# A two-layer hybrid decoder trunk on one core: one subtraction in place of two for the weight sums, three more weight units by seven products, and a convolution tap added by DMA

## The chip, the cores and the metric

The kernel runs on one core of a Trainium2 chip. The metric is the device time of one execution in microseconds (us), given as the median of several runs. Lower is better.

The engines' names in the profile are: PE is TensorE's matmuls and PEld its weight loads, DVE is VectorE, ACT is ScalarE, POOL is GpSimd, SP is SyncE. Each engine works through its own list of instructions in order and waits on semaphores of the others. DMAs issued by SP and POOL run on 16 DMA engines.

## The reference

The input is one sequence of 256 tokens with 2048 features, in float32. Layer 0 mixes tokens by causal pooling, layer 1 by an attention that merges three dilated branches. After each mixer come a residual with a layer norm, a gated feed-forward part with a causal convolution of width 3, and again a residual with a layer norm. The change touches the feed-forward part (in both layers) and the weight units that attention's value projection and the down projections share:

```python
def conv_ffn(h, w_up, conv_w, conv_b, w_down):
    S = h.shape[1]
    u = h @ w_up
    up = jnp.pad(u, ((0, 0), (CONV_WIDTH - 1, 0), (0, 0)))
    c = conv_b + up[:, 0:S] * conv_w[0]
    for j in range(1, CONV_WIDTH):
        c = c + up[:, j:j + S] * conv_w[j]
    gate, val = jnp.split(c, 2, axis=-1)
    return (jax.nn.silu(gate) * val) @ w_down
```

The inner width is 5504, that is 43 blocks of 128. All weights together are some 380 MB, and each is read once.

## The kernel before

**Weight units.** All weights go through one list, `units`. A unit is a piece of 512 x 512 of a weight matrix (1 MB; a few have 384 rows or columns). `run_units` works through the list. For unit i, `ahead(i)` first issues the load of a unit further on (SP, three tiles `raw`) and the splitting of unit i + 3, then the matmuls of unit i are issued, then what is due from `later`, then the unit's closing work.

**High and low parts.** Matmuls take their operands in a rounded form of float32. To keep precision, each weight tile is split into a high part `wh` (a cast on ACT) and a low part `wl` (the tile less its high part, a subtraction on DVE), and each product is the sum of three: high by high, high by low and low by high. A plain unit is one cast of 128 x 2048 (L99) and one subtraction (L100). There are four tiles each for `wh` and `wl`, so the splitting of a unit waits until the unit four before it has been used.

**Seven products.** In many units of the down projections and of attention's value projection, `group_tm` computes the unit's product as a 2 x 2 block product with seven block products instead of eight (`mk_seven`). Each of the seven is 2 steps of 3 matmuls of 256 columns: 42 matmuls. A plain unit of these stages is 24 matmuls of 512 columns (`go_t`, L255 to L257). A seven-product unit stands in the list as two entries, "a" (18 matmuls) and "b" (24), and both are made from one loaded tile by `split_sums`:

- "a": a cast of three quarters of the tile (L119); on DVE a difference of weight blocks (L120), the low part (L121), a second difference (L122), and the last one, over half of the tile (L124). The differences overwrite `raw`.
- "b": the overwritten tile is split again, in two halves of 128 x 1024: a cast on ACT (L113) and a subtraction on DVE (L114) for each. The first half needs L120 and L122, the second L124.

There are 72 such units before the change. `sevens` in `ffn` says which blocks q of the down projection are taken so, and for which of the four output blocks c.

**Feed-forward.** The inner blocks are taken four at a time: q = 0 to 10, the last with three. `up(q)` gives four units for the gate half and four for the value half. When the gate's last unit is through, `gate_chain` moves the result to SBUF (`evac`), and `conv` makes the convolution: the last tap with its bias on ACT (L616), then `second` one unit later and `third` two units later, each a tap on ACT (L621) and an addition on DVE (L622). Then the Silu (L644) follows on ACT, one unit after `third`. The value half goes the same way, and `valued` multiplies the two (L702). The tiles `u`, `c`, `a` and `f` share four buffers.

The down projection comes in chunks. Chunks 0 and 1 (three blocks q each) are woven between the units of `up`: in rounds of four plain units and three seven-product units, one round for each output block c. Chunk 2 has two blocks, and its two units for one c stand behind four units of `up`. The last chunk of layer 0 is done in feature order without seven products; that of layer 1 (`down(3, True)`) has blocks 8, 9 and 10.

The results of the seven-product groups are put together by DVE (L845 to L876) and then, in part, added onto the output by two accumulating DMAs of 256 KB each, issued by POOL (L287, `ht<-w`). POOL has few other instructions there. Two other DMAs, L411, accumulate 512 KB each (`h<-cs`).

**Order.** The program is written with `manual_schedule`: the order on each engine is that in which the code issues. `later(n, fn)` holds `fn` back by n entries of the list.

Of the kernel before, what the change touches and what calls it, by code (L numbers as in the profile page):

```python
# [9 lines left out]
F32 = mybir.dt.float32  # L10
# [3 lines left out]
OP = mybir.AluOpType  # L14
# [18 lines left out]
def trunk(ctx: ExitStack, tc: tile.TileContext, x, pool_w_in, pool_w_grp, pool_scale, pool_w_out,  # L33
          attn_w_q, attn_w_o, shared_w_k, shared_w_v, ffn_w_up, ffn_conv_w, ffn_conv_b, ffn_w_down,
          ln1_g, ln1_b, ln2_g, ln2_b, out):
    nc = tc.nc
    V, A, PE = nc.vector, nc.scalar, nc.tensor
# [53 lines left out]
    def do_split(i):  # L91
        if len(units[i]) > 3:
            return split_sums(i, units[i][3])
        r = raw.pop(i)
        shape = [P, r.shape[1], r.shape[2]]
        wh[i] = wp.tile(shape, F32R, name=f"wh{i}", tag="wh")
        wl[i] = wp.tile(shape, F32R, name=f"wl{i}", tag="wl")
        for j, s in enumerate(pieces(i, r.shape[1])):
            A.copy(wh[i][:, s], r[:, s])  # L99
            V.tensor_tensor(wl[i][:, s], r[:, s], wh[i][:, s].bitcast(F32), OP.subtract)  # L100
            if i == 0 and j == 0:
                x_quad(0, (1,))


    B1, B2, N1, N2 = slice(0, 4, 2), slice(1, 4, 2), slice(256, 512), slice(0, 256)

    def split_sums(i, kind):
        h = wh[i] = wp.tile([P, 4, 512], F32R, name=f"wh{i}", tag="wh")
        l = wl[i] = wp.tile([P, 4, 512], F32R, name=f"wl{i}", tag="wl")
        if kind == "b":  # L110
            r = raw.pop(i - 1)
            for n in (N2, N1):
                A.copy(h[:, :, n], r[:, :, n])  # L113
                V.tensor_tensor(l[:, :, n], r[:, :, n], h[:, :, n].bitcast(F32), OP.subtract)  # L114
            return
        r = raw[i]
        r11, r12, r22 = r[:, B1, N1], r[:, B1, N2], r[:, B2, N2]
        hs, ls, rs = (t.rearrange("p (k b) n -> p k (b n)", b=2)[:, :, 256:] for t in (h, l, r))
        A.copy(hs, rs)  # L119
        V.tensor_tensor(r12, r12, r11, OP.subtract)  # L120
        V.tensor_tensor(ls, rs, hs.bitcast(F32), OP.subtract)  # L121
        V.tensor_tensor(r22, r22, r12, OP.subtract)  # L122
        both = r[:, :, N1].rearrange("p (k b) n -> p k b n", b=2)
        V.tensor_tensor(both, both, r22.unsqueeze(2).to_broadcast([P, 2, 2, 256]), OP.subtract)  # L124
# [10 lines left out]
    def later(n, fn):  # L135
        if n == 0:
            fn()
        else:
            pending.append([n, fn])
# [418 lines left out]
    def add_grp(g):  # L558
# [12 lines left out]
             True, 0, 0, after=lambda q: to_tokens(q))  # L571
# [8 lines left out]
    def ffn(lay):  # L580
# [5 lines left out]
        sevens = {q: every for q in range(8)}  # L586
        sets = {0: "C", 1: "A", 2: "B", 3: "C", 4: "A", 5: "B", 6: "A", 7: "CB"[lay], 9: "A"}
        if lay == 1:
            sevens[9] = (0, 2)
        else:  # L590
            sevens[7] = (0, 1)
        free, done = {}, {}

        def pads():
# [4 lines left out]
        def evac(ps, nb, mode):  # L599
            u = pads()  # L600

            if mode == "x":
                norm_evac(ps, nb, lambda m: u[:, m, 2:])
                return u
            for m, n, p in pairs(ps, nb):
                y = u[:, m:m + n, 2:]
                A.copy(y, p[:, :n, T:])  # L607
                V.tensor_tensor(y, y, p[:, :n, :T], OP.add)
            return u

        def conv(u, blk0, nb, then, quick=False):
            cv = cvec[lay]
            c = pools["ffn"].tile([P, 4, T], F32, name="c", tag="t4")
            for m in range(nb):
                j = blk0 + m
                A.activation(c[:, m, :], u[:, m, 2:], AF.Identity, scale=cv[:, 2, j:j + 1], bias=cv[:, 3, j:j + 1])  # L616

            def tap(i, to):
                for m in range(nb):
                    j = blk0 + m  # L620
                    A.activation(to[:, m, :], u[:, m, i:i + T], AF.Copy, scale=cv[:, i, j:j + 1])  # L621
                V.tensor_tensor(c[:, :nb], c[:, :nb], to[:, :nb], OP.add)  # L622

            def second():
                tap(1, pools["ffn"].tile([P, 4, T], F32, name="a", tag="t4"))

            def third():
                tap(0, u[:, :, 0:T])
                then(c)

            for n, fn in ((1, second), (2, third)):
                later(0 if quick else n, fn)

        def gate_post(q, nb, mode):
            def post(ps):
                later(2 if mode == "x" else 0, lambda: gate_chain(q, nb, mode, ps))
            return post

        def gate_chain(q, nb, mode, ps):
                u = evac(ps, nb, mode)  # L640

                def gated(c):
                    def three():
                        A.activation(c[:, :nb], c[:, :nb], AF.Silu)  # L644
                        gates[q] = c

                    later(1, three)

                later(1, lambda: conv(u, 4 * q, nb, gated))

# [44 lines left out]
        def val_chain(q, nb, mode, ps):  # L697
            u = evac(ps, nb, mode)

            def valued(c):  # L700
                s = gates.pop(q)
                V.tensor_tensor(s[:, :nb], s[:, :nb], c[:, :nb], OP.mult)  # L702

                def three():
                    gq[q] = quad_tile("g")
                    split_act(gq[q], s[:, :nb])
                    if q in sevens:
                        left_sums(q, s)

                at(free.get(q, 0), three)  # L710

            after(done.get(q, 0) or state["done"] + (0 if q in (2, 5) or (q == 10 and lay == 0) else 1), lambda: conv(u, NF + 4 * q, nb, valued, q == 10))
# [57 lines left out]
        for n in (0, 1):  # L770
            d = down(n, False)
            q = chunks[n + 1][0]
# [25 lines left out]
    def to_tokens(q):  # L798
        if q == 0:
            ST["hb"] = hp.tile([P, 4, T], F32, name="hb", tag="h")  # L800
        hb = ST["hb"]
        hf = hb.rearrange("p m t -> p (m t)")
        V.transpose(hf.rearrange("p (t m c) -> p m t c", t=2, m=4), H[q].rearrange("p m (t c) -> p m t c", t=2))

        def to():
            HT[q] = hp.tile([P, 4, T], F32, name="ht", tag="h").rearrange("p a t -> p (a t)").rearrange(
                "p (t c) -> p t c", t=2)
            return HT[q].rearrange("p t c -> p (t c)")

        moves(hf, to)  # L810
# [49 lines left out]
    def tm_post(lay, n, c):  # L860
# [92 lines left out]
        return post  # L953

    ffn(0)
    marks.append(len(units))

# [174 lines left out]
    add_last(attn_w_o[0], rows4, [lambda j=j: oq[j] for j in range(4)], True, 1, 0, after=to_tokens)  # L1132
    marks.append(len(units))
    ffn(1)
    marks.append(len(units))

# [34 lines left out]
    with tc.tile_pool(name="pool", bufs=1) as pp:  # L1171
# [5 lines left out]
        for l in range(2):  # L1177
            n = 80 if l == 0 else 64
            r = pp.tile([80, P], F32, name=f"vrow{l}")
# [94 lines left out]
```

## Time and profile before

| | |
|---|---|
| time, median of 3 runs | 2016.33 us (2015.55 to 2018.14) |
| profiled execution, first to last instruction | 2014.9 us |
| PE busy | 2005.8 us |
| DVE busy | 1734.9 us |
| ACT busy | 1269.7 us |
| POOL busy | 93.0 us |
| weight loads of 1 MB from SP, issue to landing | 5.0 to 6.0 us by group (median) |
| accumulating DMAs of 256 KB from POOL (`ht<-w`), 50 | 4.8 us (median) |
| accumulating DMAs of 512 KB from POOL (`h<-cs`), 2 | 11.8 us (median) |
| granted TensorE clock | 1.000 |

The profile has only the span of the execution profiled; the median of the runs is 1.4 us above it. A row of the order of time begins with its start and its length in us, then come the engine, the line, the operation, output and inputs, and in brackets how long the engine had been idle before it and what ended that. A row of the view of groups has count, busy time, mean in ns and idle time ahead. Lines L... are those of the kernel before. The ends of matmuls are modelled, so the time that one takes is read from start to start.

### The profile page before, as it was taken

Reading aid. Unit: us, or ns where it says so; the run is one execution under the profiler, and the core shown is the slowest. Engines: PE = TensorE matmul, PEld = TensorE weight load, DVE = VectorE, ACT = ScalarE, POOL = GpSimd, SP = SyncE. Lnnn points to the kernel's source line nnn. Section 1 sums busy time; section 2 is a strip of 40 time slices with the busy share of each in tenths; the row PEclk is TensorE's granted clock in tenths of the full one; section 3 lists DMA queues with packets and bytes.
Section 4 is the critical chain, followed back from the end, with each engine's and each line's share of the span. In section 5 each row is a group of like instructions: output and inputs, shape, how many; then the busy total and the mean of one; then the engine's idle time right before and its main releaser. Section 6 shows DMA issues by size and latency. Waiting matters only on the chain.

```text
span 2014.9 us, 31474 instructions
## 1 busy us (share of the span) xinstructions
PE 2005.8 (100%) x12760; PEld 1810.2 (90%) x12760; DVE 1734.9 (86%) x1831; ACT 1269.7 (63%) x1551; POOL 93.0 (5%) x153
## 2 busy tenths in 40 slices
PE   9999999999999999999999999999999999999999
PEld 8898988999899988889888988998899989989987
DVE  6868887999899899879896878787899899989899
ACT  6454686767766676657554445487766677667673
POOL 2000000000000000000001021000000000000000
PEclk9999999999999999999999999999999999999999
DMA  8565466666666757885465656557666756666765
GB/s 260 204 208 186 163 212 192 181 221 223 198 198 200 239 179 229 232 230 186 155 220 172 210 172 202 187 188 211 166 224 200 224 186 222 209 211 186 213 208 185
DMA packets 271297, 407.77 MB, mean 202 GB/s; under 512 B 74430, under 2 KB 85588, under 8 KB 270896
## 3 DMA queue, kind: packets, MB, share of 16 engines
q1 hardware_dynamic: 259488, 388.93, 58.8%
q0 software_dynamic: 11232, 16.18, 5.4%
q8 instruction: 100, 1.64, 0.3%
q10 hardware_dynamic: 432, 0.66, 0.1%
q14 instruction: 45, 0.37, 0.1%
HBM read 380.01 MB, written 2.10 MB: 190 GB/s over the span
## 4 chain that ended last, share of the span: by engine, by line
PE 88%; DVE 7%; ACT 2%; DMA 2%; issue 1%; SPq 0%; DVEq 0%; ACTq 0%
PE acc L180 41%; PE acc L181 21%; PE s L244 3%; PE s L246 3%; PE s L245 3%; PE acc L184 2%; PE acc L185 2%; PE acc L183 2%; PE t L246 2%; PE t L244 2%; PE t L245 2%; DVE wl L100 2%; ACT wh L99 1%; DVE wl L114 1%; DVE wl L121 1%
## 5 line engine op out<-in xcount | busy, mean ns | idle before, releaser
L180 PE MATMUL acc<-xc,wh 128*128 128x512 f32 x3264 | 1151.6, 396 | 0.0
L181 PE MATMUL acc<-xc,wl 128*128 128x256 f32 x3264 | 916.2, 281 | 0.8 <-DVE wl L100 0.8
L100 DVE TENSOR_TENSOR wl<-raw,wh 128x2048 fp32r<-128x2048 f32 (+2 forms) x304 | 654.8, 2162 | 171.0 <-ACT wh L99 163.3
L180 PEld LDWEIGHTS acc<-xc,wh 128*128 128x128 f32 x3264 | 616.1, 189 | 142.8 <-issue 0.4
L99 ACT CAST wh<-raw 128x2048 fp32r<-128x2048 f32 (+2 forms) x304 | 546.6, 1805 | 170.8 <-PE acc L180 65.7
L181 PEld LDWEIGHTS acc<-xc,wl 128*128 128x128 f32 x3264 | 615.2, 188 | 1.3 <-DVE wl L100 1.2
L113 ACT CAST wh<-raw 128x1024 fp32r<-128x1024 f32 x144 | 150.7, 1052 | 202.8 <-DVE raw L122 175.5
L114 DVE TENSOR_TENSOR wl<-raw,wh 128x1024 fp32r<-128x1024 f32 x144 | 171.8, 1221 | 11.2 <-ACT wh L113 11.2
L121 DVE TENSOR_TENSOR wl<-raw,wh 128x1536 fp32r<-128x1536 f32 x72 | 126.2, 1753 | 6.3 <-ACT wh L119 5.3
L119 ACT CAST wh<-raw 128x1536 fp32r<-128x1536 f32 x72 | 106.4, 1477 | 36.6 <-PE acc L180 26.5
L287 POOL DMA_DIRECT2D ht<-w x48 | 41.3, 1015 | 1446.4 <-DVE ht L873 720.9
L244 PE MATMUL t<-wh,g 128*128 128x256 f32 x376 | 105.8, 281 | 0.0
L246 PE MATMUL t<-wh,g 128*128 128x256 f32 x376 | 105.7, 281 | 0.0
L245 PE MATMUL t<-wl,g 128*128 128x256 f32 x376 | 105.5, 281 | 0.0
L616 ACT ACTIVATE c<-u,cv 128x256 f32<-128x256 f32 x172 | 89.5, 593 | 23.2 <-DVE f L678 16.5
L246 PE MATMUL s<-wh,xs 128*128 128x256 f32 x344 | 96.1, 279 | 0.0
L244 PE MATMUL s<-wh,xs 128*128 128x256 f32 x344 | 95.9, 279 | 0.0
L245 PE MATMUL s<-wl,xs 128*128 128x256 f32 x344 | 95.9, 279 | 0.0
L124 DVE TENSOR_TENSOR raw<-raw 128x1024 f32<-128x1024 f32 x72 | 88.2, 1225 | 2.4
L621 ACT ACTIVATE a<-u,cv 128x256 f32<-128x256 f32 x172 | 73.5, 500 | 11.9 <-DVE g L688 11.9
L607 ACT COPY u<-acc 128x512 f32<-128x512 f32 x84 | 46.8, 572 | 46.1 <-PE acc L181 45.9
L621 ACT ACTIVATE u<-u,cv 128x256 f32<-128x256 f32 x172 | 73.4, 500 | 0.0
(338 smaller groups left out, 3443.1 us busy)
## 6 DMA issues: line engine op xcount, KB each, us to landing
raw<-in_ffn_w_up_dram SPq DMA_DIRECT2D x160, 1024.0 KB, 5.2
raw<-in_ffn_w_down_dram SPq DMA_DIRECT2D x80, 1024.0 KB, 5.1
raw<-in_pool_w_out_dram SPq DMA_DIRECT2D x16, 1024.0 KB, 5.0
raw<-in_shared_w_k_dram SPq DMA_DIRECT2D x16, 1024.0 KB, 5.2
raw<-in_attn_w_q_dram SPq DMA_DIRECT2D x16, 1024.0 KB, 5.3
raw<-in_shared_w_v_dram SPq DMA_DIRECT2D x16, 1024.0 KB, 5.4
raw<-in_attn_w_o_dram SPq DMA_DIRECT2D x16, 1024.0 KB, 5.2
ht<-w POOLq DMA_DIRECT2D x50, 256.0 KB, 4.8
```

Of the source, the lines that this page charges most:

```text
L99: A.copy(wh[i][:, s], r[:, s])
L100: V.tensor_tensor(wl[i][:, s], r[:, s], wh[i][:, s].bitcast(F32), OP.subtract)
L113: A.copy(h[:, :, n], r[:, :, n])
L114: V.tensor_tensor(l[:, :, n], r[:, :, n], h[:, :, n].bitcast(F32), OP.subtract)
L119: A.copy(hs, rs)
L121: V.tensor_tensor(ls, rs, hs.bitcast(F32), OP.subtract)
L180: PE.matmul(ps[m].ap, h[:, k, c], q[:, k, :, :T], start=st, stop=False)
L181: PE.matmul(ps[m][:, :T], l[:, k, c], q[:, k, 0, :T], start=False, stop=sp)
L244: PE.matmul(to, xh, h[:, k, n], start=opens and kk == 0, stop=False)
L245: PE.matmul(to, xh, l[:, k, n], start=False, stop=False)
L246: PE.matmul(to, xl, h[:, k, n], start=False, stop=ends and kk == 1)
L621: A.activation(to[:, m, :], u[:, m, i:i + T], AF.Copy, scale=cv[:, i, j:j + 1])
```

## The change

Three edits.

1. In `split_sums`, "b" is split by one cast and one subtraction of 128 x 2048 instead of two each of 128 x 1024.
2. In `ffn`, three more units are taken by seven products: block 7 in layer 0 for output blocks 2 and 3, and block 9 in layer 1 for output block 1. There are 75 such units then.
3. In `conv`, for the gate blocks alone, the addition of the third tap (22 in all) is no longer on DVE but an accumulating DMA that POOL issues (512 KB; `u` is read in rows of 1 KB). The Silu is held back by one more unit.

```diff
         if kind == "b":
             r = raw.pop(i - 1)
-            for n in (N2, N1):
-                A.copy(h[:, :, n], r[:, :, n])
-                V.tensor_tensor(l[:, :, n], r[:, :, n], h[:, :, n].bitcast(F32), OP.subtract)
+            A.copy(h, r)
+            V.tensor_tensor(l, r, h.bitcast(F32), OP.subtract)
             return
...
         if lay == 1:
-            sevens[9] = (0, 2)
-        else:
-            sevens[7] = (0, 1)
+            sevens[9] = (0, 1, 2)
...
-        def conv(u, blk0, nb, then, quick=False):
+        def conv(u, blk0, nb, then, quick=False, by_dma=False):
...
-                V.tensor_tensor(c[:, :nb], c[:, :nb], to[:, :nb], OP.add)
+                if by_dma and i == 0:
+                    nc.gpsimd.dma_start(c[:, :nb], to[:, :nb], accum_op=OP.add)
+                else:
+                    V.tensor_tensor(c[:, :nb], c[:, :nb], to[:, :nb], OP.add)
...
-                    later(1, three)
+                    later(2, three)
 
-                later(1, lambda: conv(u, 4 * q, nb, gated))
+                later(1, lambda: conv(u, 4 * q, nb, gated, by_dma=True))
```

The lines of the changed kernel are up to 3 lower than those of before until L618, and the same from L622 on (L113 and L114 become L112 and L113, L119 to L124 become L118 to L123, L287 is L286). The new DMA is L620.

What stands on VectorE in layer 0 around the fourth gate block (q = 3), before. `wl73` is the low part of a "b" entry; `raw75` is the tile of the next seven-product unit, whose entries are `wl75` and `wl76`; `c_3747` is the gate's convolution:

```order
L873 SCALAR_TENSOR_TENSOR ht_2772<-ht_2772,t_3517 128x256
L114 TENSOR_TENSOR wl73_3804<-raw72_3681,wh73_3803 128x4x256 x2
L622 TENSOR_TENSOR c_3747<-c_3747,u_3719 128x1024
L100 TENSOR_TENSOR wl74_3849<-raw74_3752,wh74_3848 128x2048
L120 TENSOR_TENSOR raw75_3801<-raw75_3801 128x2x256
L121 TENSOR_TENSOR wl75_3888<-raw75_3801,wh75_3887 128x2x768
L122 TENSOR_TENSOR raw75_3801<-raw75_3801 128x2x256
L124 TENSOR_TENSOR raw75_3801<-raw75_3801 128x4x256
L114 TENSOR_TENSOR wl76_3917<-raw75_3801,wh76_3916 128x4x256 x2
```

The same place after the change:

```order
L873 SCALAR_TENSOR_TENSOR ht_2772<-ht_2772,t_3515 128x256
L113 TENSOR_TENSOR wl73_3798<-raw72_3675,wh73_3797 128x2048
L100 TENSOR_TENSOR wl74_3841<-raw74_3746,wh74_3840 128x2048
L119 TENSOR_TENSOR raw75_3795<-raw75_3795 128x2x256
L120 TENSOR_TENSOR wl75_3879<-raw75_3795,wh75_3878 128x2x768
L121 TENSOR_TENSOR raw75_3795<-raw75_3795 128x2x256
L123 TENSOR_TENSOR raw75_3795<-raw75_3795 128x4x256
L113 TENSOR_TENSOR wl76_3909<-raw75_3795,wh76_3908 128x2048
```

The gate's addition is gone, and each low part of a "b" entry is one instruction, directly behind the last difference of its tile.

ScalarE at the same place, before:

```order
L113 CAST wh73_3803<-raw72_3681 128x4x256 x2
L621 ACTIVATE u_3719<-u_3719,cv0_583 128x256 x4
L99 CAST wh74_3848<-raw74_3752 128x2048
L644 ACTIVATE c_3747<-c_3747 128x1024
L119 CAST wh75_3887<-raw75_3801 128x2x768
L113 CAST wh76_3916<-raw75_3801 128x4x256 x2
L99 CAST wh77_3946<-raw77_3885 128x2048
```

And after:

```order
L112 CAST wh73_3797<-raw72_3675 128x2048
L618 ACTIVATE u_3713<-u_3713,cv0_583 128x256 x4
L99 CAST wh74_3840<-raw74_3746 128x2048
L118 CAST wh75_3878<-raw75_3795 128x2x768
L644 ACTIVATE c_3741<-c_3741 128x1024
L112 CAST wh76_3908<-raw75_3795 128x2048
L99 CAST wh77_3936<-raw77_3876 128x2048
```

The Silu (L644) stands one cast later, directly ahead of the cast of a "b" entry.

On POOL the DMAs of layer 0 follow each other like this after the change (`ht<-w` are the pairs that were there before, `c<-u` the new ones of the third, fourth, fifth and sixth gate block):

```order
L620 DMA c_3252<-u_3195 128x4x256
L286 DMA ht_2772<-w_3785 128x512 x2
L620 DMA c_3741<-u_3713 128x4x256
L286 DMA ht_2982<-w_4139 128x512 x2
L286 DMA ht_3178<-w_4493 128x512 x2
L620 DMA c_4449<-u_4421 128x4x256
L286 DMA ht_3389<-w_4850 128x512 x2
L620 DMA c_5094<-u_5048 128x4x256
```

Before, only the pairs stood there. The fourth and the fifth block's DMA now stand directly behind a pair.

## The prediction

> **What bounds the kernel now.** I read the page first, then TensorE's own waits, then the order of time of VectorE, ScalarE and TensorE in the stretches that the diff touches. The page's span and its line of busy times:
>
> ```profile
> span 2014.9 us, 31474 instructions
> ...
> PE 2005.8 (100%) x12760; PEld 1810.2 (90%) x12760; DVE 1734.9 (86%) x1831; ACT 1269.7 (63%) x1551; POOL 93.0 (5%) x153
> ```
>
> TensorE is busy through the whole span. Its longest entry in the view of waits is this one, at the start of the program:
>
> ```profile
> PE acc L183 <- ACT wh L99: 1.6, 1, 1.6
> ```
>
> So time is saved only where TensorE has less to do, and lost wherever a weight comes later than TensorE wants it. VectorE at 86% is the engine with little room. How little is seen in the stages that use seven products. In two rounds of these (three seven-product units and four plain ones, 37.3 us of TensorE each), and in the last 40 us of the down projection, the stretches show:
>
> ```profile
> 401.50:438.80 37.30, 37.30 (x256) 34.44 (x255) 35.16 (x33) 25.66 (x31) 1.70 (x2) 1.00 0.69 216
> 438.80:476.10 37.30, 37.30 (x256) 34.44 (x255) 35.68 (x34) 24.61 (x29) 1.70 (x2) 1.00 0.68 212
> 1944.90:1985.30 40.40, 40.40 (x218) 34.51 (x217) 38.50 (x42) 24.91 (x27) 0.00 (x0) 1.00 0.61 211
> ```
>
> The columns are stretch, length, then busy time of PE, weight loads, DVE, ACT and POOL. VectorE works 35.2, 35.7 and 38.5 us of 37.3, 37.3 and 40.4. There TensorE and VectorE are all but level, and a VectorE that waits 2 us more in a round falls behind.
>
> **Three more units by seven products.** The starts of a plain unit (24 matmuls of 512 columns, L255 to L257), and of the 18 matmuls of 256 columns of a seven-product unit's first half, in TensorE's order of time:
>
> ```profile
> 1018.02 0.39 PE L255 MATMUL t<-wh,xc 128*128 128x512 f32 x1
> ...
> 1023.59 0.28 PE L244 MATMUL s<-wh,xc 128*128 128x256 f32 x1
> ...
> 1025.72 0.59 PE L1107 MATMUL o<-pTs,vt 128*128 128x256 f32 x2
> ```
>
> A plain unit takes 1023.59 - 1018.02 = 5.57 us. The 18 take 2.13, or 0.118 each, so 42 take 4.97. Three units save 3 x 0.6 = **1.8 us** of TensorE. That is the only direct gain.
>
> **The merged low parts.** VectorE before, in a place with nothing between L124 and L114, and ScalarE at the same time:
>
> ```profile
> 404.70 0.68 DVE L120 TENSOR_TENSOR raw<-raw 128x512 f32<-128x512 f32 x1
> 405.30 1.75 DVE L121 TENSOR_TENSOR wl<-raw,wh 128x1536 fp32r<-128x1536 f32 x1
> 407.08 0.69 DVE L122 TENSOR_TENSOR raw<-raw 128x512 f32<-128x512 f32 x1
> 407.81 1.22 DVE L124 TENSOR_TENSOR raw<-raw 128x1024 f32<-128x1024 f32 x1
> 408.95 2.43 DVE L114 TENSOR_TENSOR wl<-raw,wh 128x1024 fp32r<-128x1024 f32 x2
> 411.96 2.29 DVE L100 TENSOR_TENSOR wl<-raw,wh 128x2048 fp32r<-128x2048 f32 x1 [0.58 <-ACT wh L99]
> ```
>
> ```profile
> 402.61 1.06 ACT L644 ACTIVATE c<-c 128x1024 f32<-128x1024 f32 x1 [2.52 <-DVE c L622]
> 403.58 1.46 ACT L119 CAST wh<-raw 128x1536 fp32r<-128x1536 f32 x1
> 407.86 2.26 ACT L113 CAST wh<-raw 128x1024 fp32r<-128x1024 f32 x2 [2.83 <-DVE raw L122]
> 410.02 1.90 ACT L99 CAST wh<-raw 128x2048 fp32r<-128x2048 f32 x1
> ```
>
> The halves are a pipeline. The first cast starts when L122 is done (407.77) and runs beside L124, so VectorE goes from L124 to L114 without a gap and ends at 411.38. One cast of the whole tile must wait for L124 (end 409.03), takes 1.90 (the L99 row) and ends at about 411.0; one subtraction of 2.29 follows and ends at 413.3. VectorE idles 2 us. The part is ready 1.9 us later, and the next plain unit's subtraction starts at 413.3 where it started at 411.96: 1.3 later. What the merge saves is 2.43 - 2.29, about 0.2 us with the gap between starts. Of the 75 units after the change, 40 have nothing between the two on VectorE; in the others work of about 1 us or more stands between, and I count them at nothing, less the 0.2.
>
> In a round two of the three units are bare: VectorE's 35.4 us (mean of the two rows) becomes 35.4 - 3 x 0.2 - 0.6 + 2 x 2.0 = 38.2. The 0.6 is half a gate's addition, which only every second round has. About 0.3 of its other waits stay: 38.5 against TensorE's 37.3, 1.2 us over. There are four stretches of four such rounds (two per layer). Four rounds are 4.8 over; the lead with which a part is ready before its use covers some. The use of the part made at 411.38 begins here:
>
> ```profile
> 414.23 0.28 PE L245 MATMUL s<-wl,xs 128*128 128x256 f32 x1
> ```
>
> So the lead is 2.85, and 4.8 - 2.9 = 1.9 us are lost in a stretch, **8 us** in four. Between stretches 40 us of plain units let VectorE recover.
>
> **The gate's last tap by DMA.** It takes this off VectorE, of which the gates are half:
>
> ```profile
> L622 DVE TENSOR_TENSOR c<-c,u 128x1024 f32<-128x1024 f32 (+1 forms) x44 | 52.3, 1189 | 0.5 <-ACT u L621 0.5
> ```
>
> 22 x 1.19 = 26 us of VectorE, spread over the gates. The Silu now waits for a DMA. ScalarE is in order: behind the waiting Silu stand the cast L112 (L113 before), then L99 and L118; VectorE waits for these, and TensorE for VectorE. The price of the DMA is shown only by its nearest kin, L411 (512 KB accumulated from 1 KB rows, two in a row) and L287 (256 KB, 2 KB rows):
>
> ```profile
> L411 POOL DMA_DIRECT2D h<-cs x2: 1285/1462/1639, 888.4 to 889.3; - x2
> ...
> DMA to landing us min/median/max: 10.4/11.8/13.2
> ```
>
> ```profile
> DMA to landing us min/median/max: 3.3/4.8/8.4
> ```
>
> In 8 of the 22 gates (fourth, fifth, seventh and eighth block of each layer) the new DMA stands on POOL right behind an L287 pair. For the fourth block of layer 0 the pair is issued here:
>
> ```profile
> 399.43 1.79 POOL L287 DMA_DIRECT2D ht<-w  x2 [316.56 <-DVE ht L873]
> ```
>
> The new one follows at about 400.9. Its bounds are 4.8 (landing 405.7) and 13.2 (414.1). It is L411's shape with 512 KB ahead of it in the queue, but the pair has a head start; I take 9.1, nearer to L411's 10.4, so 410.0. The Silu then runs to 411.05. Without its addition VectorE ends L124 1.2 earlier, at 407.8, and the whole cast could start then; it starts at 411.05. That is 3.1 us late, and in a stretch with no room it costs all of it: 8 x 3.1 = **25 us**. The other gates have no pair ahead and over 8 us to the Silu's new place; I count them at nothing, apart from the ninth block, which is in the next term.
>
> The Trainium skill, "DMA: Bandwidth & Descriptors", section "Anatomy of one DMA — SWDGE (gpsimd) path", fits such a DMA by 2.0 us and its bytes at 436 GB/s: an estimate of 3.2 us for 512 KB. By that the DMA lands near 404.1 and the 25 fall away; L411's 10.4 us in this trace speaks against it.
>
> **Groups of the third down chunk.** Two seven-product units follow each other there, once per output block, eight times in all. VectorE, ScalarE and TensorE in the second group of layer 0:
>
> ```profile
> 768.14 2.42 DVE L114 TENSOR_TENSOR wl<-raw,wh 128x1024 fp32r<-128x1024 f32 x2
> 770.47 1.24 DVE L831 STREAM_TRANSPOSE hb<-ht 128x1024 f32<-128x1024 f32 x1
> ...
> 777.06 2.35 DVE L114 TENSOR_TENSOR wl<-raw,wh 128x1024 fp32r<-128x1024 f32 x2
> 780.83 2.29 DVE L100 TENSOR_TENSOR wl<-raw,wh 128x2048 fp32r<-128x2048 f32 x1 [1.42 <-ACT wh L99]
> ```
>
> ```profile
> 776.92 2.08 ACT L616 ACTIVATE c<-u,cv 128x256 f32<-128x256 f32 x4
> 778.90 1.89 ACT L99 CAST wh<-raw 128x2048 fp32r<-128x2048 f32 x1
> ```
>
> ```profile
> 783.62 0.28 PE L181 MATMUL acc<-xc,wl 128*128 128x256 f32 x1
> ```
>
> The last part is ready at 783.12, 0.5 us before its use. The first L114 comes 1.8 later (bare), the second another 0.8, and the casts L616 and L99 wait behind it: the cast of 778.90 starts at 781.8 and its subtraction ends at 786.0. TensorE loses 2.4 us. Over eight groups with leads like this or a little larger, and the ninth block's Silu among them, I take 1.75 each: **14 us**. Two of the new seven-product units lie here; they add VectorE work of 4.5 us each (the five rows above, 6.7, less a plain 2.2).
>
> **Attention's second value group.** Three seven-product units follow each other. VectorE's last part of them, and TensorE after it:
>
> ```profile
> 1035.85 2.40 DVE L114 TENSOR_TENSOR wl<-raw,wh 128x1024 fp32r<-128x1024 f32 x2
> ```
>
> ```profile
> 1039.95 0.40 PE L180 MATMUL acc<-xc,wh 128*128 128x512 f32 x1
> 1041.19 0.38 PE L181 MATMUL acc<-xc,wl 128*128 128x256 f32 x1 [0.84 <-DVE wl L100]
> ```
>
> TensorE already loses 1.0 us at 1039.95, and has no lead. Two bare units make the last part 4 us later: **+4 us**.
>
> **The tail.** The third new unit stands in the last stretch above: 38.5 + 4.5 + 1.3 (one bare unit) + 1.5 (more additions for its products, an estimate) = 45.8 us of VectorE for 39.8 of TensorE. With a lead of about 1 us, **+5 us**.
>
> **Sum.** -1.8 + 8 + 25 + 14 + 4 + 5 = +54. The execution profiled spans 2014.9, the median of three runs is 2016.33, so 1.4 us lie around the span and stay: 2016.3 + 54 is about **2070 us**.
>
> **Rivals.** (1) The DMA lands before the Silu's turn: the 25 fall away, and 2 of the 14: 2070 - 27 = 2043. For it: L287's 4.8, and two units' time before the Silu. Against: L411. (2) Faster: VectorE loses 26 us of additions and 75 x 0.2 of merging, and if the bare waits fit into its lead everywhere, TensorE runs through: 2016.3 - 1.8 - 1.0 (the gap at 1039.95) = 2013.5. It decides at 783.62: the lead there must exceed the 2.9 us by which the walk makes the part later, and it is 0.5. (3) No change that can be told: the stalls stay at 2 or 3 us in attention and the tail. (4) TensorE's clock drops in its new waits: a half at half pace doubles 24 x 0.118 = 2.8 us, and with eight such waits the time is 2070 + 23 = 2093. The stretches above grant 1.00 throughout, with no long gap to test it. The Trainium skill, "TensorE: Matmul & The Clock Gate", section "Part 1: The HAM clock gate", says that an idle window of about 3.4 us halves the clock; no run here shows that yet.
>
> **Chances.** Forecast 0.52 (2045 to 2090 by its landing time), rival 1 0.25, rival 4 0.07, a loss of 5 to 12 us 0.05, rival 3 0.05, rival 2 0.06. About 0.2% (4 us) is what a measurement of this kernel tells from no change. Faster 0.06, same 0.05, slower 0.89. The range goes from 2028, below rival 1, to 2095, above rival 4; the DMA's 13.2 would go past it.
>
> **What would show it.** Right: the profile after has L113 on VectorE idle for about 2 us <- ACT wh L112 some 40 times; Silu L644 idle <- DMA c<-u, 2 to 4 us in eight places; TensorE waiting for DVE wl; landings of c<-u of 8 to 11 us. Wrong: landings under 6 us, no wait of TensorE for wl, or L113 following L123 without a gap.

## The result and the profile after

The changed kernel takes 2162.44 us (median of 5 runs, 2159.11 to 2166.14) against 2016.34 us before (5 runs): a ratio of 1.0724, with a 95% interval of 1.0711 to 1.0737. It is 146 us slower, where 54 us were forecast. The direction was right; the size was not, and the time lies above the range.

The page's span and its line of busy times, after:

```profile
span 2160.6 us, 31503 instructions
...
PE 2054.8 (95%) x12814; PEld 1845.8 (85%) x12814; DVE 1719.7 (80%) x1754; ACT 1259.1 (58%) x1483; POOL 121.9 (6%) x175
```

The span is 145.7 us longer. TensorE, which was idle for 2014.9 - 2005.8 = 9.1 us, is now idle for 105.8; and its busy time is 49.0 us longer, though it has less to multiply. So two thirds of the loss are gaps and one third is busy time. Part of that third is a lower clock, shown below: 300 matmuls start while the granted clock is at a half, and at 0.21 us each instead of 0.12 that is about 27 of the 49 us, an estimate. The rest stays open; a matmul counts as busy for 0.28 us where the next starts 0.12 us later, so short waits can hide in it. VectorE and ScalarE both have less work than before. What they wait for is in the view of waits (engine, line, what it waited for; total, times, longest):

```profile
ACT wh L112 <- DVE raw L123: 242.1, 54, 7.9
DVE wl L113 <- ACT wh L112: 161.7, 57, 9.6
ACT c L644 <- DMA c<-u: 128.5, 18, 12.2
PE s L243 <- ACT wh L112: 43.6, 13, 5.3
PE s L244 <- DVE wl L113: 37.1, 30, 2.6
```

All the waits that the forecast named are there: the merged cast (L112) for the last difference (L123), the merged subtraction (L113) for the cast, the Silu (L644) for the DMA, TensorE for the parts. The Silu's wait is too long: 7.1 us on average, up to 12.2, in 18 gates, where 2 to 4 us in eight were forecast.

The stretch of the fourth gate of layer 0, which the forecast walked through, on ScalarE, VectorE and TensorE:

```profile
403.24 1.48 ACT L118 CAST wh<-raw 128x1536 fp32r<-128x1536 f32 x1
416.24 1.06 ACT L644 ACTIVATE c<-c 128x1024 f32<-128x1024 f32 x1 [11.53 <-DMA c<-u]
417.20 1.88 ACT L112 CAST wh<-raw 128x2048 fp32r<-128x2048 f32 x1
```

```profile
408.93 1.23 DVE L123 TENSOR_TENSOR raw<-raw 128x1024 f32<-128x1024 f32 x1
419.12 2.29 DVE L113 TENSOR_TENSOR wl<-raw,wh 128x2048 fp32r<-128x2048 f32 x1 [8.96 <-ACT wh L112]
```

```profile
414.22 0.28 PE L245 MATMUL t<-wh,g 128*128 128x256 f32 x1
419.14 0.58 PE L243 MATMUL s<-wh,xs 128*128 128x256 f32 x1 [4.64 <-ACT wh L112]
421.46 0.58 PE L244 MATMUL s<-wl,xs 128*128 128x256 f32 x1 [1.75 <-DVE wl L113]
421.84 0.42 PE L245 MATMUL s<-wh,xs 128*128 128x256 f32 x1
422.06 0.41 PE L243 MATMUL s<-wh,xs 128*128 128x256 f32 x1
```

The chain can be read backwards: TensorE waits for the cast, the cast stands behind the Silu, the Silu waits for the DMA. The cast could have started at 410.2, when L123 was done, and starts at 417.2. TensorE loses 4.64 + 1.75 = 6.4 us of idle time, and afterwards its matmuls start 0.21 us apart instead of 0.12. The view of stretches shows why (the column after POOL's busy time is the granted clock):

```profile
409.00:414.00 5.00, 5.00 (x36) 4.59 (x35) 1.15 (x1) 0.00 (x0) 0.00 (x0) 1.00 1.14 285
414.00:417.00 3.00, 0.50 (x5) 0.29 (x3) 0.00 (x0) 0.76 (x1) 0.00 (x0) 1.00 0.44 126
417.00:422.00 5.00, 1.11 (x3) 0.83 (x4) 2.88 (x2) 5.00 (x4) 0.00 (x0) 0.51 0.00 0
422.00:427.00 5.00, 5.00 (x25) 4.90 (x24) 4.93 (x5) 0.26 (x1) 0.00 (x0) 0.50 0.91 326
```

The last matmul before the wait ends at 414.5. The clock is full until shortly after 417, then drops to a half (0.51 on average from 417 to 422) and stays there until 427. The Trainium skill, "TensorE: Matmul & The Clock Gate", section "Part 1: The HAM clock gate", says that an idle window of about 3.4 us halves the clock: this trace agrees on the halving, which comes after 2.6 us here.

The DMA itself, by its line, from issue to landing over all 22 gates:

```profile
L620 POOL DMA_DIRECT2D c<-u x22: 1259/1285/1975, 269.6 to 2065.9; - x22
...
DMA to landing us min/median/max: 5.6/10.5/14.1
```

In the eight gates behind a pair of ht transfers (L286 here) it takes 12.3 to 14.1 us, in the other fourteen 5.6 to 11.6.

### The profile page after: what moved, and what is told of

The parts are those of the page before. It is cut to its first block, busy times and chain, and to the rows that moved or that the text cites. A ratio compares the mean times of both kernels' runs of the same rounds, so it can differ in the third digit from the quotient of the medians.

```text
span 2160.6 us, 31503 instructions
## 1 busy us (share of the span) xinstructions
PE 2054.8 (95%) x12814; PEld 1845.8 (85%) x12814; DVE 1719.7 (80%) x1754; ACT 1259.1 (58%) x1483; POOL 121.9 (6%) x175
## 5 line engine op out<-in xcount | busy, mean ns | idle before, releaser
L112 ACT CAST wh<-raw 128x2048 fp32r<-128x2048 f32 x75 | 142.9, 1906 | 276.4 <-DVE raw L123 242.1
L113 DVE TENSOR_TENSOR wl<-raw,wh 128x2048 fp32r<-128x2048 f32 x75 | 171.8, 2290 | 161.7 <-ACT wh L112 161.7
L243 PE MATMUL s<-wh,xs 128*128 128x256 f32 x362 | 109.6, 303 | 42.1 <-ACT wh L112 42.0
L244 PE MATMUL s<-wl,xs 128*128 128x256 f32 x362 | 112.5, 311 | 33.8 <-DVE wl L113 33.8
L118 ACT CAST wh<-raw 128x1536 fp32r<-128x1536 f32 x75 | 110.8, 1477 | 28.3 <-DMA raw<-in_ffn_w_down_dram 14.9
L243 PE MATMUL t<-wh,g 128*128 128x256 f32 x396 | 114.7, 290 | 0.0
L245 PE MATMUL t<-wh,g 128*128 128x256 f32 x396 | 114.2, 289 | 0.0
L244 PE MATMUL t<-wl,g 128*128 128x256 f32 x396 | 114.1, 288 | 0.0
L243 PEld LDWEIGHTS s<-wh,xs 128*128 128x128 f32 x362 | 74.7, 206 | 44.7 <-ACT wh L112 44.7
L244 PEld LDWEIGHTS s<-wl,xs 128*128 128x128 f32 x362 | 75.2, 208 | 41.0 <-DVE wl L113 40.6
L245 PE MATMUL s<-wh,xs 128*128 128x256 f32 x362 | 108.4, 299 | 0.0
L644 ACT ACTIVATE c<-c 128x1024 f32<-128x1024 f32 (+1 forms) x22 | 22.9, 1039 | 128.6 <-DMA c<-u 128.5
L123 DVE TENSOR_TENSOR raw<-raw 128x1024 f32<-128x1024 f32 x75 | 91.9, 1225 | 2.6
L286 POOL DMA_DIRECT2D ht<-w x48 | 41.7, 1024 | 868.9 <-ACT u L618 540.8
```

The lines of the kernel that those rows point to most:

```text
L112: A.copy(h, r)
L113: V.tensor_tensor(l, r, h.bitcast(F32), OP.subtract)
L243: PE.matmul(to, xh, h[:, k, n], start=opens and kk == 0, stop=False)
L244: PE.matmul(to, xh, l[:, k, n], start=False, stop=False)
L245: PE.matmul(to, xl, h[:, k, n], start=False, stop=ends and kk == 1)
```

## The experiments

**The three parts, each alone, and two together.** Theory A at this point: the DMA's late landing in eight gates is most of the loss. Theory B: the merge is, because it takes VectorE's room everywhere.

The merge alone:

```
-            for n in (N2, N1):
-                A.copy(h[:, :, n], r[:, :, n])
-                V.tensor_tensor(l[:, :, n], r[:, :, n], h[:, :, n].bitcast(F32), OP.subtract)
+            A.copy(h, r)
+            V.tensor_tensor(l, r, h.bitcast(F32), OP.subtract)
```

> Before with the merged cast and subtraction of the low parts alone. Theory A (the changed kernel loses most by the accumulating DMA, which lands 12.3 to 14.1 us after its issue in eight gates and holds the casts behind the Silu): the merge accounts for the gaps of TensorE away from those gates, 50 us of 113 with some reduced clock after them, part of which belongs to the three new units: 2016 + 35 to 50, about 2058, with few gaps in the four-round stretches and most in the groups of the third down chunk and in attention. Theory B (the merge is the main cost, since it takes VectorE's room everywhere, and the late Silu only shows where that room is gone): 2016 + 80 to 100, about 2105. The forecast's own terms for the merge (8 + 14 + 4 + part of 5) give 2016 + 28 = 2044.

The DMA alone (with `later(2, three)` for the Silu):

```
+                if by_dma and i == 0:
+                    nc.gpsimd.dma_start(c[:, :nb], to[:, :nb], accum_op=OP.add)
...
```

> Before with the gate's last tap by the accumulating DMA, and the Silu one unit later, alone; cast and subtraction in halves as before. Theory A: the DMA still lands 12 to 14 us after issue in the eight gates behind a pair of ht transfers, TensorE waits there for the half cast (0.95 us sooner than the whole one) and the half subtraction: about 3.7 + 1.2 us in each, some 5 of 8 with reduced clock after it: 2016 + 40 to 58, about 2066. Theory B: with the halves VectorE has the room to absorb the late Silu: at most 2030, TensorE's gaps at the eight places under 2 us.

The three units alone:

```
-            sevens[9] = (0, 2)
-        else:
-            sevens[7] = (0, 1)
+            sevens[9] = (0, 1, 2)
```

> Before with the three more units by seven products alone. Theory A and the forecast: 3 x 0.6 us less of TensorE, 2014.5. Rival: VectorE has no room for 4.5 us more work per unit where they lie (lead 0.5 us in the third down chunk, about 1 us in the tail): each unit costs 1 to 3 us instead, 2018 to 2023.

Merge and units together, without the DMA: the first and the third edit.

> The changed kernel without the DMA: merge and the three new units, the gate's last tap added by VectorE again, Silu at its old place. Theory A: 2058 to 2065, so that the DMA on top of these is worth some 100 us, of which about 9 us (6.6 idle, 2.3 at half clock) stands in each of eight gates and 4 to 5 in each of the two ninth gates. Theory B: 2110 or more, the DMA worth under 50. If the costs of the parts add up, this is the first plus the third run less 2016.

| kernel | us | ratio (95% interval) | over before, us |
|---|---|---|---|
| merge | 2082.80 | 1.0328 (1.0310 to 1.0345) | +66.4 |
| DMA | 2085.69 | 1.0348 (1.0332 to 1.0363) | +69.3 |
| three units | 2026.50 | 1.0052 (1.0037 to 1.0067) | +10.1 |
| merge and units | 2097.24 | 1.0400 (1.0384 to 1.0415) | +80.9 |
| all | 2162.44 | 1.0724 (1.0711 to 1.0737) | +146.1 |

The three add up to 145.8, the whole is 146.1. That fit is closer than the measurements are (each interval is some 3 us either way), and merge and units together cost 80.9 where their sum is 76.5; so all that can be said is that no interaction of the parts shows clearly. Neither theory holds as it was put. The merge and the DMA cost about the same, and the units, forecast as the only gain, cost 10 us.

How the merge costs, in VectorE's order of time in the kernel with the merge alone, and in one of its rounds:

```profile
450.94 1.23 DVE L123 TENSOR_TENSOR raw<-raw 128x1024 f32<-128x1024 f32 x1
454.19 2.29 DVE L113 TENSOR_TENSOR wl<-raw,wh 128x2048 fp32r<-128x2048 f32 x1 [2.03 <-ACT wh L112]
...
461.72 1.23 DVE L123 TENSOR_TENSOR raw<-raw 128x1024 f32<-128x1024 f32 x1
465.27 2.29 DVE L113 TENSOR_TENSOR wl<-raw,wh 128x2048 fp32r<-128x2048 f32 x1 [2.33 <-ACT wh L112]
```

```profile
448.00:487.20 39.20, 38.23 (x254) 34.63 (x254) 34.05 (x30) 24.85 (x27) 1.71 (x2) 1.00 0.60 188
```

The two bare units of a round idle VectorE for 2.03 and 2.33 us, as forecast, and its busy time of 34.05 in a round is the forecast's 34.2. But its waits come to 39.20 - 34.05 = 5.2 us where 4.3 were counted, and the round takes 39.2 us instead of 37.3. To see what all rounds of a layer lose, compare the same matmul in both kernels, at the first unit of layer 0's rounds and after their end. Before:

```profile
364.22 0.28 PE L245 MATMUL s<-wl,g 128*128 128x256 f32 x1
...
707.77 0.28 PE L181 MATMUL acc<-xc,wl 128*128 128x256 f32 x1
```

With the merge:

```profile
365.86 0.28 PE L244 MATMUL s<-wl,g 128*128 128x256 f32 x1
...
725.45 0.28 PE L180 MATMUL acc<-xc,wl 128*128 128x256 f32 x1
```

The distance grows from 343.55 to 359.59: 16.0 us. The same reading gives 16 in layer 1's rounds, 15 in the two third down chunks together, 8.5 in attention's value group and 5.4 in the tail.

**Is it VectorE's idle time?** One subtraction, but the cast in halves, so that the first half runs early:

```
             for n in (N2, N1):
                 A.copy(h[:, :, n], r[:, :, n])
+            V.tensor_tensor(l, r, h.bitcast(F32), OP.subtract)
```

> Before with one subtraction of the whole low part, but the cast still in two halves, the first of which runs beside L124 of before. Theory (the merge costs by the idle time of VectorE between the last difference and the merged subtraction, 2.0 to 2.3 us in a bare unit, since the whole cast of 1.9 us starts only after that difference): the idle falls to about 1.1 us (a half cast of 0.95), a four-unit round of 37.3 us is no longer short of VectorE, the 33 us lost in the rounds fall to about 4, attention and the third down chunk to half: 2016 + 18 = 2034 (2026 to 2042). Rival (the part being ready in one piece and 1 us later is what hurts, not VectorE's idle time): 2016 + 45 or more.

Measured: 2037.92 us, ratio 1.0103 (1.0087 to 1.0118), +21.4: as the theory had it. VectorE in the place of the first of the two waits above:

```profile
447.42 1.22 DVE L124 TENSOR_TENSOR raw<-raw 128x1024 f32<-128x1024 f32 x1
449.77 2.29 DVE L114 TENSOR_TENSOR wl<-raw,wh 128x2048 fp32r<-128x2048 f32 x1 [1.12 <-ACT wh L113]
```

The idle time falls from 2.03 to 1.12, and the price of the merge from 66 to 21 us. The bare unit shown has 0.9 us less of idle time, and two thirds of the loss are gone.

**Only the covered units.** The merge in the 33 units of 72 in which VectorE has other work in between:

```
+            covered = (63, 66, 73, 83, 93, 111, 114, 121, 131, 141, 157, 159, 167, 174, 181, 210, 217, 236, 297, 300, 307,
...
+            for n in (slice(0, 512),) if i in covered else (N2, N1):
```

> Before with the merge in only 33 of its 72 units, those in which VectorE has other work between the last difference and the subtraction; the 39 bare ones keep their halves. Theory, and the forecast's claim (covered units cost nothing): 2015 to 2019. Rival (a cast of 1.9 us in one piece costs in ScalarE's order too, wherever it stands): 2016 + 15 to 30, the rest of the 66 us of the first run.

Measured: 2021.59 us, ratio 1.0026 (1.0015 to 1.0037), +5.1. "Nothing" is a little low. By subtraction 61 of the 66 us are the 39 bare units'; the merge in these alone was not run.

**Only the gates without a pair.** The DMA in 14 gates; the eight others as before:

```
+                    later(1 if q in (3, 4, 6, 7) else 2, three)
...
+                later(1, lambda: conv(u, 4 * q, nb, gated, by_dma=q not in (3, 4, 6, 7)))
```

> Before with the accumulating DMA in the 14 gates that have no pair of ht transfers ahead of theirs; the eight others keep VectorE's addition and their Silu's old place. The forecast counted these 14 at nothing but for the ninth blocks (two of 1.75 us): 2016 to 2021. What the second run's order of time shows at their places (8.8 and 7.3 us at the ninth blocks, 2 to 4 at the sixth, tenth and eleventh): 2016 + 25 = 2041 (2034 to 2048).

Measured: 2033.70 us, ratio 1.0082 (1.0067 to 1.0097), +17.2: under the 25 expected, but not nothing. It lies at the two ninth blocks (5.1 and 2.5 us by the same matmul in both kernels), the wait for the row sums at the end of layer 0 (3.0) and in small pieces of layer 1's tail; 1.4 us stand at the start of the program, ahead of all these DMAs. By subtraction the eight gates are left with 69.3 - 17.2 = 52 us. A closer reading is by the two matmuls named above, and by the same ones of layer 1, between which the eight gates lie: the rounds take 343.55 and 343.53 us in the two layers, before and in this kernel alike, and 365.14 and 366.49 with the DMA in all gates. That is 44.6 us, or 5.6 for each of the eight. The rest is at the two ninth blocks, which cost 8.8 and 7.3 us with the DMA in all gates.

**What makes the DMA late.** In the kernel with the DMA alone, the pair of ht transfers is issued four units later, behind the gate's DMA:

```
-                    nc.gpsimd.dma_start(y, z, accum_op=OP.add)
+                    later(4, lambda y=y, z=z: nc.gpsimd.dma_start(y, z, accum_op=OP.add))
```

In layer 0's third chunk these additions then reach ht after it has been transposed, so that part of the computation is changed.

> The kernel of the second run (DMA alone, halves kept) with the pair of ht transfers issued four units later, behind the gate's DMA instead of ahead of it in the queue. Queue theory (the 512 KB of the pair ahead cost the eight gates 3 to 4 us): they land 9.5 to 10.5 us after issue like the gates without a pair in the busy stretches, the Silu idles about 8 us instead of 11 to 12, TensorE's gaps there shrink by some 3 us: 2086 - 20 to 28 = 2062. Rival (the weight loads alone set the landing): 12 to 14 us as before and 2083 to 2088.

Measured: 2064.47 us, ratio 1.0234 (1.0219 to 1.0249), 21 us under the DMA alone. By its line and in the window of the fourth gate:

```profile
L623 POOL DMA_DIRECT2D c<-u x1: 1256/1256/1256, 398.5 to 398.5; - x1
...
DMA to landing us min/median/max: 5.6/5.6/5.6
```

In all eight gates it lands after 5.3 to 7.0 us, better than the queue theory had it. How much the eight gates gain is read from the same two matmuls of layer 0. With the DMA alone:

```profile
365.90 0.28 PE L245 MATMUL s<-wl,g 128*128 128x256 f32 x1
...
731.04 0.28 PE L181 MATMUL acc<-xc,wl 128*128 128x256 f32 x1
```

With the pair behind:

```profile
363.19 0.28 PE L245 MATMUL s<-wl,g 128*128 128x256 f32 x1
...
708.86 0.28 PE L181 MATMUL acc<-xc,wl 128*128 128x256 f32 x1
```

The distance falls from 365.14 to 345.67 us, and in layer 1 from 366.49 to 345.85: of the 44.6 us lost in the rounds, 40.2 are gone. The whole gains only 21, because another part became longer: from the end of layer 0's rounds to one matmul at the end of that layer (at 900.05 us before) it is 226.39 us, against 205.14 with the DMA alone. The late additions stand in that part; what exactly they delay there stays open.

The packets by queue show what the order of the DMAs changes: KB whose packets began in each microsecond, by the DMAs of POOL (ht pair and gate) and by the weight loads of SP, in the changed kernel's fourth gate (issue at 402.81) and in this kernel's (issue at 398.50). Some rows are left out.

```
changed kernel                             pair behind
us    POOL  weights                        us    POOL  weights
403    162     0   (ht pair)               399      0     0
405    106    48   (ht pair)               400    103     0   (gate)
407     12   304                           401    166     0   (gate)
408      0   390                           402    153     0   (gate)
409     76   212   (gate)                  403    184     0   (gate, then ht pair)
410    101   168   (gate)
412     91   186   (gate)
414     60   232   (gate)
```

Alone, the gate's 512 KB move at 150 KB per us and more once they are under way. Behind the pair they meet the next weight load: for two us (407 and 408) hardly anything but the load moves, and then the two share, with as many packets of 1 KB as of 2 KB (91 and 93 in the row of 412), so the gate gets 91 KB per us against 186. In this gate the pair costs not so much its own 4 us as the quiet slot between two loads. The Trainium skill, "DMA: Bandwidth & Descriptors", section "Anatomy of one DMA — SWDGE (gpsimd) path", gives 3.2 us for 512 KB by its fit, an estimate; the lowest here is 5.3.

**Silu held back.** The changed kernel, with the Silu of the eight gates three units later:

```
-                    later(2, three)
+                    later(5 if q in (3, 4, 6, 7) else 2, three)
```

> The changed kernel with the Silu of the eight gates (fourth, fifth, seventh and eighth block of each layer) three units later, so that it stands behind three more casts and about 10 us after its old turn; nothing else moved. Theory A (the price of the DMA is the wait of ScalarE, strictly in order, ahead of a cast that TensorE needs): landings stay at 12 to 14 us, the Silu idles under 3 us, the gaps of 4 to 5 us at these eight places go, the merge's own 1 to 2 us per round stay: 2162 - 45 = 2117 (2105 to 2125). Theory B (the DMA's traffic costs, by slowing the weight loads): 2150 or more.

Measured: 2118.44 us, ratio 1.0504 (1.0489 to 1.0520): 44 us less than the changed kernel, at the expected value. The DMA lands as late as before (11.9 to 14.2 us in these gates); what has gone is the wait of the casts. ScalarE, for the same gate:

```profile
410.20 1.91 ACT L112 CAST wh<-raw 128x2048 fp32r<-128x2048 f32 x1 [5.54 <-DVE raw L123]
412.01 1.91 ACT L99 CAST wh<-raw 128x2048 fp32r<-128x2048 f32 x1
417.30 1.48 ACT L118 CAST wh<-raw 128x1536 fp32r<-128x1536 f32 x1 [3.38 <-DMA raw<-in_ffn_w_down_dram]
418.68 1.06 ACT L644 ACTIVATE c<-c 128x1024 f32<-128x1024 f32 x1
```

The same with the DMA alone, halves kept, and the Silu held back in the later blocks too:

```
+                    later({3: 5, 4: 5, 6: 5, 7: 5, 8: 3, 9: 3, 10: 3}.get(q, 2), three)
```

> The kernel of the second run (DMA alone, halves kept) with the Silu held back by three more units in the eight gates and by one more in the ninth to eleventh blocks. Theory A: no Silu waits where a cast is due, VectorE has 26 us less to do: 2014 to 2020, level with before. Theory B (traffic): 2035 or more, with Silu waits under 3 us but TensorE's gaps still there.

Measured: 2028.62 us, ratio 1.0060 (1.0045 to 1.0075). Of the DMA's 69 us, 57 were the Silu's place. In the eight gates the DMA lands as late as ever, 11.5 to 14.3 us after its issue, and yet the rounds take 346.41 and 344.35 us: 40.9 of the 44.6 us are gone. So in the rounds it is the wait on ScalarE that costs, and not the traffic. The remaining 12 us are more than the 4 expected at most; 6.7 of them stand at the end of layer 0, where TensorE waits for the last gate's product and for the row sums. Whether that is the transfers' traffic or the order on ScalarE wasn't told apart there.

**The clock.** The changed kernel, with 32 matmuls of zeros in each of the eight gaps:

```
+                if kind == "b" and state["done"] in (76, 96, 124, 144, 312, 332, 360, 380):
+                    for _ in range(32):
+                        PE.matmul(ps[0][:, 256:512].rearrange("p (r c) -> p r c", c=16), x[:, 0, 0, :P], zero.to_broadcast([P, 16, 16]), start=False, stop=False)
...
```

> The changed kernel with 32 matmuls of 256 columns (zeros, added to a sum that is open) ahead of the matmuls of the eight second halves that wait 4 to 5 us for their cast: 3.8 us of TensorE at full clock, inside a gap that is there anyway; then no idle stretch there exceeds 2.5 us. Clock theory (the half clock after those gaps, some 23 matmuls of 0.21 instead of 0.12 us each, is paid in full): 2162 - 8 x 2.3 = 2144, and the granted clock in 410 to 430 us is 1.00. Rival (after the gap VectorE sets the pace, so a slow TensorE is hidden there): 2158 to 2163 with the clock at 1.00.

Measured: 2157.78 us, ratio 1.0700 (1.0682 to 1.0718): 4.7 us less, not 18. In the fourth gate of layer 0 the clock stayed up; in the fifth (the third row of each) it did so only in part. The changed kernel first, then this one:

```profile
410.00:420.00 10.00, 5.08 (x33) 4.32 (x31) 1.04 (x2) 3.76 (x3) 0.00 (x0) 0.85 0.59 151
420.00:430.00 10.00, 8.54 (x41) 8.08 (x42) 7.88 (x7) 4.28 (x4) 0.00 (x0) 0.63 0.58 210
505.00:515.00 10.00, 8.25 (x39) 7.64 (x39) 8.30 (x6) 4.28 (x3) 0.00 (x0) 0.62 0.59 210
```

```profile
410.00:420.00 10.00, 8.30 (x63) 7.67 (x61) 1.38 (x1) 4.27 (x3) 0.00 (x0) 1.00 0.54 138
420.00:430.00 10.00, 9.04 (x61) 8.31 (x62) 7.88 (x7) 4.28 (x4) 0.00 (x0) 1.00 0.59 210
505.00:515.00 10.00, 7.63 (x41) 6.96 (x41) 8.68 (x6) 4.28 (x4) 0.00 (x0) 0.83 0.59 208
```

In the changed kernel the clock is at a half for 6.8 or 10.2 us at each of the eight gates, and 188 matmuls start in that time. Here it stays full at three of them and is at a half for 3.4 us at the other five, with 77 matmuls. So the test took away 111 of 188 slow matmuls, about 10 us at 0.09 us each (an estimate), and under half of that shows in the time, whose interval is some 3 us either way. The full price of the clock stays open. In the fourth gate, VectorE does exactly the same in 420 to 430 (7.88 us, 7 instructions) in both kernels, so the faster TensorE does not move it forward.

**The last of the three units alone:** only the change of `sevens[9]`.

> Before with only the last of the three new units by seven products, in layer 1's last chunk. If the 10 us of the three units alone belong to VectorE's want of room at the end of each layer's down projection in like measure: 2016 + 4 to 6 (a gap of about 2.5 us at the close), the other two units in layer 0 being worth the other 4 to 6. If only layer 0's two cost (before the wait for the row sums there): 2015.5.

Measured: ratio 1.0039 (1.0023 to 1.0055), +8 us, more than the 4 to 6 expected. So the unit in layer 1's last chunk seems to have most of the 10 us, and the two in layer 0 the small rest; the intervals are too wide to say more. VectorE and TensorE at its end:

```profile
1987.05 3.94 DVE L100 TENSOR_TENSOR wl<-raw,wh 128x1536 fp32r<-128x1536 f32 x2
1991.47 2.29 DVE L100 TENSOR_TENSOR wl<-raw,wh 128x2048 fp32r<-128x2048 f32 x1 [0.48 <-ACT wh L99]
```

```profile
1988.85 0.50 PE L256 MATMUL t<-wl,g 128*128 128x512 f32 x1 [2.35 <-DVE wl L100]
```

```profile
1944.60:1990.00 45.40, 41.94 (x240) 35.90 (x239) 43.87 (x52) 25.22 (x29) 0.00 (x0) 1.00 0.52 176
```

VectorE has 43.9 us of work in 45.4, and TensorE waits for it. No kernel that was run is under before: with TensorE at 100% there was nothing to gain but the 1.8 us of three units, less than a measurement tells.

## Why the forecast was wrong in size

**Three units, -1.8:** wrong in sign, +10.1. The sum took TensorE's saving as free and put the price of the extra VectorE work only into the merge's terms, though the stretch quoted had VectorE at 38.5 of 40.4 us already. The 45.8 us of VectorE that the forecast worked out for the tail (44.5 without the 1.3 of the merge) named that price: 43.9 were measured with the new unit alone.

**The merged low parts, 8:** 32 us in the rounds. The mechanism and the 2.0 us of idle per bare unit were right; two steps of the sum failed. The round is over by 1.9 us (39.2 less 37.3), not 1.2. And the lead of 2.85 us was credited to each of the four stretches, since "Between stretches 40 us of plain units let VectorE recover". That does not hold: by the same matmul in both kernels, the first stretch of layer 0 loses 5.8 us (4 x 1.9, less a lead of about 2) and the second 9.4, as if it had no lead; the 1.8 us by which 9.4 exceeds 4 x 1.9 stay open. Attention cost 8.5, not 4: TensorE waited at two second halves (1.5 and 4.1 us) and not only at the last part, and behind the second wait its matmuls started 0.21 us apart, which is about 2 us more. The third down chunks and the tail lose 15 and 5.4 by the merge alone, where 14 and 5 were to cover the new units and the ninth block's Silu too. The covered units, counted "at nothing", are 5 us in 33 of the units of before.

**The gate's DMA, 25:** 69 us, of which 44.6 are in the rounds with the eight gates, 17 are there without these, and the rest is at the ninth blocks. The failed step is the landing time: "I take 9.1" where the bounds were 4.8 and 13.2, and 12.3 to 14.1 came. The head start given to the pair was the error: the pair's transfer was over by 407, but it had used up the slot before the next weight load. The path that the forecast named (DMA, Silu, cast, part, TensorE) holds: with an early landing, or with the Silu moved out of it, over 40 of the 44.6 us go. With a landing at 416.2 (4.3 us of the 6.2 are the landing time, 1.9 the issue, at 402.8 instead of 400.9) the walk gives a cast (416.2 + 1.1 - 411.05) + 3.1 = 9.3 us late. A second error of the walk hides behind the first: it charged the whole delay and took off no lead. Less the lead of 2.85, the 9.3 come to about 6.5, near the 6.4 measured in this gate (with the merge) and the 5.6 per gate (without it); but the forecast's own 3.1 would have come to 0.3. The 25 was a sum of two errors of opposite sign. The other gates, "at nothing", were the smaller miss.

**The rivals.** The DMA in time (1) fell: it lands nearly in time only without the pair ahead, and then most of the loss in the rounds goes. The clock (4) came true in the trace at all eight gates, some 23 matmuls at half pace in each. Its price of 18 to 23 us looks too high: taking away about 10 us of slow matmuls gained 4.7. As the clock was held up only in part, the price itself stays open.

**What would show it:** L113 idle behind L112 (57 times, 2.8 us on average, for some 40 times and 2), TensorE waiting for the parts: right. Silu waits of 2 to 4 us in eight places and landings of 8 to 11: too low.

## What to carry to other kernels

An instruction that waits for a DMA on an in-order engine costs what stands behind it, so put the wait behind the next work that others need: three units' delay was worth 44 us here, and in the eight gates no cost of it shows. Merging two halves of a chain that crosses two engines saves 0.2 us of fixed cost and loses the overlap of 2 us; count it against the idle time of the engine that has no room. And where a bound has two ends far apart, look at what else the queue and the DMA engines carry in that very microsecond before taking the middle.

## What the runs showed of the hardware that was not expected

- The same 512 KB accumulating DMA lands 5.3 us after its issue between two weight loads and 14.1 us behind a pair and beside a load. In the fourth gate it is served packet for packet beside a load, so 1 KB packets get half the bytes of 2 KB ones (91 against 186 KB per us).
- After an idle time of 4.6 us the granted clock was 0.50 for about 10 us, from 2.6 us after the last matmul to about 6 us after matmuls came without gaps again. Over the eight gates it was at a half for 6.8 or 10.2 us each; keeping 111 of the 188 matmuls concerned at the full clock was worth 4.7 us of 146.
- A transfer that lands 11.5 to 14.3 us after its issue cost 44.6 us in the rounds when a Silu ahead of a due cast waited for it, and 3.7 when the Silu stood three units later.
